# Hybrid decoder block: two delta heads' keys and queries kept on chip, attention's outputs stored whole, convolution's zeros by ScalarE

## The chip, the cores and the metric

The kernel runs on one core of one Trainium2 chip. Its time is that of one launch in microseconds on the device, as a median of several runs. The profile is one further execution, recorded by the hardware profiler. In its rows PE is TensorE's matmuls, PEld its weight loads, DVE is VectorE, ACT ScalarE, POOL GpSimd, SP SyncE; SPq marks what SP issues, which here is nearly every DMA.

## The reference

One decoder block over 1024 tokens of width 1024 in float32: a norm, one input projection, two groups of heads side by side (8 heads of stick-breaking attention of width 64, 4 heads of gated DeltaNet of width 128), their norms and gates, one output projection, the residual and a last norm.

```python
h = rmsnorm(x, norm1_w[layer])
proj = jnp.einsum('btd,de->bte', h, w_in[layer])
sb_q, sb_k, sb_v, sb_z, g_q, g_k, g_v, g_z, g_b, g_a = jnp.split(proj, split_idx, axis=-1)
o_sb = stick_breaking_attention(to_heads(sb_q, SB_HEADS, SB_HEAD_DIM),
                                to_heads(sb_k, SB_HEADS, SB_HEAD_DIM),
                                to_heads(sb_v, SB_HEADS, SB_HEAD_DIM))
o_sb = rmsnorm(o_sb.transpose(0, 2, 1, 3), sb_norm_w[layer]).reshape(b, t_len, SB_WIDTH)
o_sb = o_sb * jax.nn.silu(sb_z)
qkv = jax.nn.silu(causal_depthwise_conv(jnp.concatenate([g_q, g_k, g_v], axis=-1), gdn_conv_w[layer]))
gq, gk, gv = jnp.split(qkv, 3, axis=-1)
gq = l2norm(to_heads(gq, GDN_HEADS, GDN_HEAD_DIM)).astype(x.dtype)
gk = l2norm(to_heads(gk, GDN_HEADS, GDN_HEAD_DIM)).astype(x.dtype)
o_gdn = gated_delta_chunked(gq, gk, gv, decay, beta)
o_gdn = rmsnorm(o_gdn.transpose(0, 2, 1, 3), gdn_norm_w[layer]).reshape(b, t_len, GDN_WIDTH)
o_gdn = o_gdn * jax.nn.silu(g_z)
mixed = jnp.concatenate([o_sb, o_gdn], axis=-1)
x = x + jnp.einsum('bte,ed->btd', mixed, w_out[layer])
return rmsnorm(x, final_norm_w)
```

The convolution has four taps along time: each output needs the three inputs before it, and the first three of a sequence are zeros.

## The kernel before

**A planner writes the order.** The kernel is built by streams (Python generators, started at the end of `block`) that yield whenever they wait. `interleave` picks the stream that may go on and has the lowest rank; for the engines other than TensorE, `Model` (lines 176 to 345) keeps a simulated clock. Every instruction is recorded with a modelled cost and a rank `ck.prio`; of those that are ready in the model, the one of the lowest rank is taken next (`Model.start`). The orders found so are fixed by dependencies, so each engine runs its instructions in just that order. SP is one such engine, "S": it issues the DMAs one after the other, 0.475 us each in the model, and one whose data isn't there holds up all behind it. Ranks are given in line 37: DELTA 0, WEIGHTS 2, BANK 5, WINDOW 10, OUTPUT 12, RESULT 20. Since each instruction is issued by one helper (`call`, line 363), all rows of the profile have that line; they are told apart by the names of their tiles.

**Precision.** Most matmuls are made of three with operands split in a high and a low part (`mm3`): xh and xl are the split input, weh and wel a split column of weights, wer the raw column, each loaded in two halves.

**Stages.** Up to some 73 us the first projections (attention's queries and values) run while the input comes in. Then `projections` works through the other columns in `ORDER`: G0 to G3 are a delta head's keys, queries and values (kinds 1, 0, 2), k0 to k3 attention's keys, z the gates. Its rank, 100, makes it fill TensorE wherever delta and attention have nothing to do. From 531 us the output projection follows: 8 blocks of 128 rows with the delta half of the weights (`products_delta`), then 8 with attention's half (`products_attention`).

**Delta heads.** `g_evac` (line 878) takes a column out of PSUM in two halves of 512 tokens: ScalarE copies it to pre, behind three columns that are zeros (half 0, VectorE's memset, line 885) or the last three of the half before (ScalarE); the four taps give ac, in one of two buffers tagged kt; GpSimd multiplies ac by its sigmoid. Heads 0 and 1 (`TURNED` = 2) store the result to g_s as it is. Heads 2 and 3 store keys and queries to g_s as well, and all three kinds turned, by VectorE's transpose and four DMAs to gt_s.

`delta_load` (line 991) fetches, for each head and half (a unit), keys and queries from g_s into a slot kq of [128, 4 chunks, 2, 128]. There are four such slots; in the beginning they hold the raw input xr0 to xr3, and at the end the block inputs mg. `gdn_pre` turns keys and queries of heads 0 and 1 on TensorE (tile kw, the same bytes as kq), takes their norms (nkv) and the products kqf; it fetches its decays as cb and dt. All units' decays are computed ahead of the first unit, in the same stream. `gdn_chain` is the scan over the chunks, which ends with four stores to og_s.

**Attention.** `window` handles 256 queries of one head. z = q·k goes through sigmoids and a scan (sg, cc), is turned, split (ahl) and multiplied with the head's values v2a, a single tile loaded anew for each head when the last window of the head before has used it. The result, o2, is turned in 32x32 blocks by VectorE into oe, [128, 256], and stored to o_s by four DMAs of 32 partitions, 128 bytes a run, so that o_s holds token rows. Queries, keys high and low are loaded per head as q, kh, kl from qk_s; `k_evac` writes the keys there through the one tile sqh and a kt buffer, and `z_evac` uses the same two tiles.

**After attention.** `out_norm` loads one block of 128 rows from o_s (512 KB, whole rows) into a tile named both, adds the two halves of each head, and computes the norms. Its loads wait until the last window's stores are recorded. The loads for the delta half of the output projection (mgf from og_s and gate_s), the weights (worf) and x again (xr) run on SP in the same time.

Of the kernel before, what the change touches and what calls it, by code (L numbers as in the profile page):

```python
# [10 lines left out]
F32 = mybir.dt.float32  # L11
F32R = mybir.dt.float32r
I32 = mybir.dt.int32
AF = mybir.ActivationFunctionType
ALU = mybir.AluOpType
AX = mybir.AxisListType

P = 128
T = 1024
# [3 lines left out]
SBH = 8  # L23
# [8 lines left out]
TURNED = 2  # L32
# [1 line left out]

OUT_WEIGHTS, DELTA, WEIGHTS, BANK, WINDOW, OUTPUT, RESULT, DECAYS = -1, 0, 2, 5, 10, 12, 20, 25


SAME = 130  # L40
# [438 lines left out]
def block(tc, xT_d, x_d, n1_d, wE_d, wQ_d, wC_d, conv_d, alog_d, dtb_d, mixw_d, wo_d, fnw_d, out_d):  # L479
    nc = tc.nc  # L480
    ck = Model({"V": nc.vector, "A": nc.scalar, "G": nc.gpsimd, "P": nc.tensor, "S": nc.sync})
    V, A, G, TE, S = ck.V, ck.A, ck.G, ck.P, ck.S

    with ExitStack() as top:
        top.enter_context(tc.manual_schedule(engines={mybir.EngineType.PE}))

        def open_pool(name, space="SB", ctx=top, before=(), **kw):
            if space != "SB":
                kw["space"] = getattr(bass.MemoryType, space)
            return Pool(ck, ctx.enter_context(tc.tile_pool(name=name, bufs=1, **kw)), space, before)  # L490

        fx = Fixed(ck, nc, {**{f"sg{w}": (2048 * (w + 1), 1) for w in range(4)}, "o2": (1024, 1), "kq": (4096, 4), "ak": (4096, 4)})
        cst = open_pool("cst")
        dr = open_pool("dr", "DRAM")
# [13 lines left out]
        step = stepr.bitcast(F32)  # L508
# [7 lines left out]
        half = cst.tile([P, SBH], F32, name="half")  # L516
# [5 lines left out]
        def rsqrt(y, a, n):  # L522
            return G.tensor_tensor(y, a, half[:, 0:n], ALU.pow)
# [10 lines left out]
        gate_s = dr.tile([NK, P, T], F32, name="gate_s")  # L534
        g_s = dr.tile([GH, 3, P, T], F32, name="g_s")
        gt_s = dr.tile([GH, 3, T, P], F32, name="gt_s")
        o_s = dr.tile([T, SBH, P], F32, name="o_s")
        og_s = dr.tile([NB, P, GH, P], F32, name="og_s")
        rs_s = dr.tile([NB, P], F32, name="rs_s")
        cum_s = dr.tile([2, GH, NB, P], F32, name="cum_s")  # L540
# [16 lines left out]
        def turned(tp, parts):  # L557
            ck.hold(tp)
            for u, a in enumerate(parts):
                if a.dtype == F32R:  # L560
                    TE.transpose(tp[:, u * P:(u + 1) * P].bitcast(F32R), a, idr)
                else:
                    TE.transpose(tp[:, u * P:(u + 1) * P], a, ident)
            ck.free(tp)
            yield from ()
# [58 lines left out]
        for tag, bufs in (("kh", 1), ("kl", 1), ("q2", 1), ("v2a", 1), ("sg2", 1), ("cc", 2), ("cc", 2), ("sg3", 1)):  # L624
            if tag[0] == "s":
                chl.append(fx.tile([P, 2, 520], F32R, "chl", tag))
            else:
                t = at_.tile([P, 1040 + (48 if tag == "kl" else 0)], F32R, tag=tag, bufs=bufs, name="chl")
# [15 lines left out]
        raw, loads = [], {}  # L644
        for k in range(NK):
            w = s0.tile([P, 512], F32, tag="wcr", bufs=6, name="wq")
# [76 lines left out]
        def first(f, *args, bank=BANK, **kw):  # L723
            ck.prio, prio = bank, ck.prio
            f(*args, **kw)
            ck.prio = prio
# [49 lines left out]
        flags = {}  # L776
# [88 lines left out]
        def z_evac(i):  # L865
# [9 lines left out]

            return evac

        def g_evac(h, kind):
            wv = conv[:, 4 * kind + h, :]
            last = []  # L880

            def evac(pt, half):
                pre = gd.tile([P, 515], F32, tag="pre", bufs=2, name="pre")
                if half == 0:
                    V.memset(pre[:, 0:3], 0.0)
                else:
                    A.activation(pre[:, 0:3], last[0][:, 512:515], AF.Copy)
                last.append(pre)
                first(A.activation, pre[:, 3:515], pt, AF.Copy)
                ac = pr.tile([P, 512], F32, tag="kt", bufs=2, name="ac")  # L890

                first(A.activation, pt, pre[:, 0:512], AF.Copy, scale=wv[:, 0:1])
                for i in range(1, 4):
                    first(V.scalar_tensor_tensor, ac if i == 3 else pt, pre[:, i:i + 512], wv[:, i:i + 1], pt, ALU.mult, ALU.add)
                sg = pre[:, 0:512]
                first(A.activation, sg, ac, AF.Sigmoid)
                first(G.tensor_tensor, ac, ac, sg, ALU.mult)
                ts = slice(half * 512, half * 512 + 512)
                if h < TURNED:
                    return S.dma_start(g_s[h, kind, :, ts], ac)  # L900
                done = [S.dma_start(g_s[h, kind, :, ts], ac)] if kind < 2 else []
                first(V.transpose, sg, ac)
                turned = gt_s[h, kind, ts, :].rearrange("(b r) d -> r b d", r=32)
                return done + [S.dma_start(turned[:, :, 32 * a:32 * a + 32], sg[32 * a:32 * a + 32, :].rearrange("r (b c) -> r b c", c=32)) for a in range(4)]

            return evac

# [83 lines left out]
        def delta_load():  # L991
            yield lambda: "dec" in flags
            for h in range(GH):
                for g in range(2):
                    u = 2 * h + g
                    gst[h, g] = {}
                    half = "" if g else ".0"
                    yield lambda: u < 4 or f"c{u - 4}" in flags
                    if u > 3:
                        yield flags[f"c{u - 4}"]  # L1000
                    kq = fx.tile([P, 4, 2, P], F32, "kq", "kq")
                    ts = slice(512 * g, 512 * g + 512)
                    loads = []
                    for kind in (1, 0):
                        yield lambda: f"G{h}{kind}{half}" in flags
                        loads.append(S.dma_start(kq[:, :, 1 - kind, :], g_s[h, kind, :, ts].rearrange("p (c t) -> p c t", c=4)))
                    ak = fx.tile([P, 2, 4, P], F32, "ak", "ak")
                    kn, at = ak[:, 0], ak[:, 1]
                    nkv = gd.tile([P, 4, P], F32, tag="nkv", bufs=4, name="nkv")
                    gst[h, g].update(kq=kq, kn=kn, nkv=nkv, at=at)  # L1010
                    ck.hold(kq, kn, nkv)
                    turned = lambda kind: gt_s[h, kind, ts, :].rearrange("(c t) d -> t c d", t=P)
                    if h >= TURNED:
                        loads += [S.dma_start(kn, turned(1)), S.dma_start(nkv, turned(0))]
                    flags[f"l{u}g"] = loads
                    yield lambda: f"G{h}2{half}" in flags and (u == 0 or f"q{u - 1}" in flags)
                    vt = gd.tile([P, 4, P], F32 if h >= TURNED else F32R, tag="vt", name="vt")
                    flags[f"v{u}g"] = S.dma_start(vt, turned(2)) if h >= TURNED else S.dma_start(vt.rearrange("p c t -> p (c t)").bitcast(F32), g_s[h, 2, :, ts])
                    gst[h, g].update(vt=vt)
# [307 lines left out]
        def window(h, w, tok):  # L1327
# [3 lines left out]
            for i in range(2):  # L1331
                b = 2 * w + i
                end = (b + 1) * P
                sg = sg2[:, i, :]
                cc = ccs[i][:, T - end:T + 1]
                cuts = (0, 384, end) if end == 640 else (*range(0, end, 512), end)
                for s0, s1 in list(zip(cuts, cuts[1:]))[::-1]:
                    n = s1 - s0
# [19 lines left out]
            for j in range(w + 2):  # L1358
                if j <= w:
# [3 lines left out]
                    n = len(blocks)  # L1363
# [11 lines left out]
                    r = V.tensor_tensor(al, src, ah.bitcast(F32), ALU.subtract)  # L1375
# [13 lines left out]
                ahl, r = parts[j - 1]  # L1389
                ov2 = ov.rearrange("p (m t) -> p m t", m=2)  # L1390
                yield r
                for s in (2 * (j - 1), 2 * (j - 1) + 1):
                    i0 = 0 if s <= 2 * w else 1
                    c = slice(256 * (s % 2), 256 * (s % 2) + (1 if i0 else 2) * P)
# [10 lines left out]
            busy["po"] = 0  # L1405
            oe = at_.tile([P, 256], F32, tag="oe", bufs=2, name="oe")
            V.transpose(oe, o2)
            rows_o = o_s[256 * w:256 * w + 256, h].rearrange("(b r) d -> r b d", r=32)
            flags[f"e{h}{w}"] = [S.dma_start(rows_o[:, :, 32 * a:32 * a + 32], oe[32 * a:32 * a + 32].rearrange("r (b c) -> r b c", c=32)) for a in range(4)]
            yield  # L1410


# [2 lines left out]
        def out_norm(n):  # L1415
            yield lambda: f"e{SBH - 1}3" in flags and fx.room("sg3")
            if n == 0:
                fx.part("sg3", 4096)
            for b in range(n, NB, 2):
                yield lambda: fx.room("sg3")  # L1420
                both = fx.tile([P, SBH, 2, SBD], F32, "both", "sg3")
                ck.hold(both)
                yield S.dma_start(both.rearrange("p h u d -> p (h u d)"), o_s[b * P:(b + 1) * P].rearrange("t h d -> t (h d)"))
                o, spare = both[:, :, 0, :], both[:, :, 1, :]
                V.tensor_tensor(o, o, spare, ALU.add)
                A.activation(spare, o, AF.Square)
                ss = at_.tile([P, SBH], F32, tag="oss", bufs=2, name="oss")
                V.tensor_reduce(ss, spare, AX.X, ALU.add)
                V.tensor_scalar(ss, ss, 1.0 / SBD, EPS, ALU.mult, ALU.add)
                rsqrt(ss, ss, SBH)  # L1430
                normed[b] = both, o, ss
                yield
# [203 lines left out]
        pre = Stream(delta_pre(), 0.7, DELTA + 0.7)  # L1636
# [43 lines left out]
```

## Time and profile before

| | |
|---|---|
| runs shown | 636.03, 637.17, 634.78 us, median 636.03 |
| the profiled execution | 639.53 us; its span from first to last instruction 637.8 us |
| mean granted TensorE clock | 0.994 |
| instructions | 11259 |
| DMA | 165563 packets, 120.21 MB, 188 GB/s in the mean; 96448 packets under 512 B |

The span leaves out what lies around the first and the last instruction, 1.7 us. A busy PE in this profile isn't PE at its peak: matmuls overlap, and the end of each is modelled. In the views quoted below, a row of a tile gives the engine, the operation, its count, and min/median/max in ns with the first and last start; a row of the timeline gives the start, the duration and the instruction, with the idle time before it and who ended it in brackets; a row of waits gives who waited for whom, the sum, how often and the longest.

### The profile page before, as it was taken

To read this page: it belongs to the slowest core of one execution; us is meant where nothing else is said; L and a number is where in the kernel's file an instruction comes from. 1 tells how busy PE (TensorE), PEld (TensorE's weight loads), DVE (VectorE), ACT (ScalarE), POOL (GpSimd) and SP (SyncE) were. 2 spreads that over 40 slices of the span, in tenths; PEclk is the share of its full clock that TensorE was granted. 3 is DMA by queue.
4 is the path that set the end of the run, shared out by engine and by line. 5 is a ranking of instruction groups with operands and counts; after the bars stand their busy time and mean duration, and the time that the engine had idled before them with its cause. 6 is when DMAs were issued, how large, how long until landed. Compare 5 with 4: busy or idle time off the path is not lost.

```text
span 637.8 us, 11259 instructions
## 1 busy us (share of the span) xinstructions
PE 624.0 (98%) x3672; PEld 528.7 (83%) x3672; DVE 447.5 (70%) x810; ACT 393.9 (62%) x945; POOL 341.2 (53%) x429
## 2 busy tenths in 40 slices
PE   8999999999999999999999989999999999999995
PEld 7889988988888888788888777888888888888884
DVE  4379973322797798887797696777889774478754
ACT  6665567724786776775785866666777653232553
POOL 0124047728794696881679684386764325245522
PEclk9999999999999999999999999899999999999998
DMA  8958337856557466598668768453652578984322
GB/s 305 342 183 312 124 131 253 303 189 222 159 151 224 131 185 134 141 207 221 167 146 224 185 133 264 121 185 94 180 141 84 151 201 255 311 319 143 116 100 100
DMA packets 165563, 120.21 MB, mean 188 GB/s; under 512 B 96448, under 2 KB 131456, under 8 KB 165504
## 3 DMA queue, kind: packets, MB, share of 16 engines
q1 hardware_dynamic: 165216, 119.29, 62.3%
q8 instruction: 29, 0.48, 0.3%
q14 instruction: 30, 0.25, 0.1%
q10 hardware_dynamic: 288, 0.20, 0.1%
HBM read 80.22 MB, written 39.23 MB: 187 GB/s over the span
## 4 chain that ended last, share of the span: by engine, by line
PE 81%; DMA 6%; ACT 4%; DVE 3%; SPq 2%; issue 2%; POOL 1%; POOLq 0%; DVEq 0%; ACTq 0%
PE pp L363 52%; PE pz L363 21%; PE po L363 6%; PE pc L363 3%; SPq L363 2%; DVE cc L363 1%; DMA v2a<-v_s 1%; DMA kh<-qk_s 1%; DMA xr1f<-xT 1%; DMA o_s<-oe 1%; ACT sgf L363 1%; POOL ac L363 1%; DMA qk_s<-sqh 1%; ACT pz L363 1%; DMA cb<-cum_s 1%
## 5 line engine op out<-in xcount | busy, mean ns | idle before, releaser
L363 PE MATMUL pp<-xh,weh 128*128 128x512 f32 x360 | 146.4, 407 | 0.4 <-DVE ac L363 0.4
L363 PE MATMUL pp<-xh,wel 128*128 128x512 f32 x360 | 141.8, 394 | 0.0
L363 PE MATMUL pp<-xl,weh 128*128 128x512 f32 x360 | 141.3, 392 | 0.0
L363 POOL TENSOR_TENSOR sgf<-sgf,cc 128x128 f32<-128x128 f32 (+3 forms) x64 | 77.5, 1216 | 57.7 <-DVE cc L363 52.5
L363 POOL TENSOR_TENSOR wel<-wer,weh 128x512 fp32r<-128x512 f32 x48 | 62.5, 1305 | 72.0 <-ACT weh L363 71.6
L363 PEld LDWEIGHTS pp<-xh,wel 128*128 128x128 f32 x360 | 68.0, 189 | 15.3
L363 PEld LDWEIGHTS pp<-xh,weh 128*128 128x128 f32 x360 | 68.1, 189 | 12.8 <-DVE ac L363 0.9
L363 PEld LDWEIGHTS pp<-xl,weh 128*128 128x128 f32 x360 | 68.1, 189 | 11.5
L363 DVE TENSOR_TENSOR_SCAN cc<-pz,step 128x384 f32<-128x384 f32 (+2 forms) x64 | 53.4, 844 | 10.6 <-ACT pz L363 9.5
L363 ACT ACTIVATE sgf<-pz,rs 128x384 f32<-128x384 f32 (+3 forms) x96 | 53.5, 593 | 7.6 <-PE pz L363 7.6
L363 DVE TENSOR_TENSOR ahl<-pz,ahl 128x512 fp32r<-128x512 f32 (+1 forms) x80 | 49.5, 630 | 12.0 <-ACT ahl L363 11.3
L363 ACT ACTIVATE ahl<-pz 128x512 fp32r<-128x512 f32 (+1 forms) x80 | 43.2, 559 | 20.6 <-PE pz L363 20.1
L363 ACT ACTIVATE pz<-pz,ns 128x384 f32<-128x384 f32 (+3 forms) x96 | 52.5, 576 | 0.0
L363 PE MATMUL po<-ahl,v2a 128*128 128x512 f32 (+1 forms) x160 | 48.9, 400 | 2.4 <-DMA v2a<-v_s 2.3
L363 PE MATMUL pp<-wo,mmf 128*128 128x512 f32 x192 | 45.5, 396 | 0.0
L363 DVE SCALAR_TENSOR_TENSOR pp<-pre,conv,pp 128x512 f32<-128x512 f32 x42 | 31.4, 747 | 18.2 <-ACT pp L363 17.8
L363 PEld LDWEIGHTS pp<-wo,mmf 128*128 128x128 f32 x192 | 35.8, 188 | 8.4
L363 PE MATMUL pp<-woh,mmf 128*128 128x512 f32 (+2 forms) x136 | 41.9, 385 | 0.0
L363 DVE TENSOR_TENSOR_SCAN cc<-pz,cc,step 128x512 f32<-128x512 f32 (+1 forms) x32 | 38.8, 1211 | 4.1 <-ACT pz L363 3.0
L363 POOL TENSOR_TENSOR mmf<-mgf,mmf 128x512 fp32r<-128x512 f32 x16 | 21.9, 1366 | 37.0 <-ACT mmf L363 23.9
L363 POOL TENSOR_TENSOR ac<-ac,pre 128x512 f32<-128x512 f32 x24 | 31.0, 1293 | 16.3 <-ACT pre L363 10.9
L363 DVE TENSOR_TENSOR xr<-pp,xr 128x512 f32<-128x512 f32 (+2 forms) x33 | 22.2, 672 | 23.0 <-PE pp L363 23.0
(317 smaller groups left out, 1513.9 us busy)
## 6 DMA issues: line engine op xcount, KB each, us to landing
wer<-wE SPq DMA_DIRECT2D x48, 256.0 KB, 3.5
xr<-x SPq DMA_DIRECT2D x16, 512.0 KB, 7.6
g_s<-ac SPq DMA_DIRECT2D x20, 256.0 KB, 2.3
v_s<-v2e SPq DMA_DIRECT2D x16, 256.0 KB, 3.3
kqf<-g_s SPq DMA_DIRECT2D x16, 256.0 KB, 4.0
v2a<-v_s SPq DMA_DIRECT2D x8, 512.0 KB, 5.9
q<-qk_s SPq DMA_DIRECT2D x8, 512.0 KB, 4.5
kh<-qk_s SPq DMA_DIRECT2D x8, 512.0 KB, 3.9
```

The costliest lines, as they stand in the source:

```text
L363: ins = f(*args, **kw).ins
```

## The change

Five edits, in four places:

1. A new rank, STORES = 1.
2. Keys and queries of heads 0 and 1 are no longer stored to g_s and loaded again. `operand(h, g)` hands out the slot kq of a unit when its first product is made, and GpSimd's product writes straight into it, with a stride. The values of these heads go to g_s as before.
3. The stores of heads 2 and 3 (to g_s and gt_s) get the rank STORES in place of RESULT.
4. o_s is laid out as [4 windows, 8 heads, 128, 256]: a window's result oe is stored as it stands, by one DMA with 1 KB a partition. The order by token is made by the loads of `out_norm`: four for a block, each for 32 partitions, 128 bytes a run.
5. The three zero columns of pre are written by ScalarE, copied from a tile that holds zeros (step).

```diff
-OUT_WEIGHTS, DELTA, WEIGHTS, BANK, WINDOW, OUTPUT, RESULT, DECAYS = -1, 0, 2, 5, 10, 12, 20, 25
+OUT_WEIGHTS, DELTA, STORES, WEIGHTS, BANK, WINDOW, OUTPUT, RESULT, DECAYS = -1, 0, 1, 2, 5, 10, 12, 20, 25
...
-        o_s = dr.tile([T, SBH, P], F32, name="o_s")
+        o_s = dr.tile([4, SBH, P, 256], F32, name="o_s")
...
+        operands = {}
+
+        def operand(h, g):
+            if (h, g) not in operands:
+                operands[h, g] = fx.tile([P, 4, 2, P], F32, "kq", "kq")
+                ck.hold(operands[h, g])
+            return operands[h, g]
...
                 if half == 0:
-                    V.memset(pre[:, 0:3], 0.0)
+                    A.activation(pre[:, 0:3], step[:, 0:3], AF.Copy)
...
+                ts = slice(half * 512, half * 512 + 512)
+                if h < TURNED and kind < 2:
+                    kq = operand(h, half)
+                    ck.prio, prio = BANK, ck.prio
+                    r = G.tensor_tensor(kq[:, :, 1 - kind, :], ac.rearrange("p (c t) -> p c t", c=4), sg.rearrange("p (c t) -> p c t", c=4), ALU.mult)
+                    ck.prio = prio
+                    return r
                 first(G.tensor_tensor, ac, ac, sg, ALU.mult)
-                ts = slice(half * 512, half * 512 + 512)
                 if h < TURNED:
                     return S.dma_start(g_s[h, kind, :, ts], ac)
+                ck.prio, prio = STORES, ck.prio
                 done = [S.dma_start(g_s[h, kind, :, ts], ac)] if kind < 2 else []
                 first(V.transpose, sg, ac)
                 turned = gt_s[h, kind, ts, :].rearrange("(b r) d -> r b d", r=32)
-                return done + [S.dma_start(turned[:, :, 32 * a:32 * a + 32], sg[32 * a:32 * a + 32, :].rearrange("r (b c) -> r b c", c=32)) for a in range(4)]
+                done += [S.dma_start(turned[:, :, 32 * a:32 * a + 32], sg[32 * a:32 * a + 32, :].rearrange("r (b c) -> r b c", c=32)) for a in range(4)]
+                ck.prio = prio
+                return done
...
-                    kq = fx.tile([P, 4, 2, P], F32, "kq", "kq")
+                    kq = operand(h, g)
...
-                        loads.append(S.dma_start(kq[:, :, 1 - kind, :], g_s[h, kind, :, ts].rearrange("p (c t) -> p c t", c=4)))
+                        loads.append(flags[f"G{h}{kind}{half}"] if h < TURNED else S.dma_start(kq[:, :, 1 - kind, :], g_s[h, kind, :, ts].rearrange("p (c t) -> p c t", c=4)))
...
-            rows_o = o_s[256 * w:256 * w + 256, h].rearrange("(b r) d -> r b d", r=32)
-            flags[f"e{h}{w}"] = [S.dma_start(rows_o[:, :, 32 * a:32 * a + 32], oe[32 * a:32 * a + 32].rearrange("r (b c) -> r b c", c=32)) for a in range(4)]
+            flags[f"e{h}{w}"] = S.dma_start(o_s[w, h], oe)
...
-                yield S.dma_start(both.rearrange("p h u d -> p (h u d)"), o_s[b * P:(b + 1) * P].rearrange("t h d -> t (h d)"))
+                loads = []
+                for q in range(4):
+                    at = 32 * (4 * (b % 2) + q)
+                    loads.append(S.dma_start(both[32 * q:32 * q + 32].rearrange("p h u d -> p (h u d)").rearrange("p (n c) -> p n c", c=32),
+                                             o_s[b // 2, :, :, at:at + 32].rearrange("h (a r) c -> r (h a) c", r=32)))
+                yield loads
```

More of the change, by code (lines that the diff above doesn't have):

```diff
@@ L1010, in delta_load @@
                     gst[h, g].update(kq=kq, kn=kn, nkv=nkv, at=at)
-                    ck.hold(kq, kn, nkv)
+                    ck.hold(kn, nkv)
                     turned = lambda kind: gt_s[h, kind, ts, :].rearrange("(c t) d -> t c d", t=P)
```

## The prediction

> **What bounds the kernel now.** I read the page first, its busy times and the shares of the chain that ended last.
>
> ```profile
> PE 624.0 (98%) x3672; PEld 528.7 (83%) x3672; DVE 447.5 (70%) x810; ACT 393.9 (62%) x945; POOL 341.2 (53%) x429
> ...
> PE 81%; DMA 6%; ACT 4%; DVE 3%; SPq 2%; issue 2%; POOL 1%; POOLq 0%; DVEq 0%; ACTq 0%
> ```
>
> The reader sees a kernel that TensorE bounds: 13.8 of 637.8 us are all that it stands idle, and no part of the change removes a matmul. What can be won is inside the waits, so the view of waits for PE comes next (who waited for whom, total us, times, longest).
>
> ```profile
> PE po L363 <- DMA v2a<-v_s: 2.3, 1, 2.3
> PE po L363 <- DVE step L363: 1.7, 1, 1.7
> PE pz L363 <- ACT wy L363: 1.5, 1, 1.5
> PE pz L363 <- DVE cc L363: 0.6, 2, 0.4
> PE pp L363 <- DVE ac L363: 0.4, 1, 0.4
> PE pz L363 <- ACT nkv L363: 0.3, 1, 0.3
> PE pz L363 <- DVE state L363: 0.2, 1, 0.2
> ```
>
> The second row is the start of the kernel, which the change doesn't touch. The other six sum to 5.3 us: the whole pool that earlier data can empty. 3.8 us of it are two waits, and for these I asked the timeline of SP (the queue that issues nearly all DMAs, one after the other) and the chain in order of time (start us, us, what).
>
> ```profile
> 348.71 2.15 SPq L363 DMA_DIRECT2D o_s<-oe  x4
> ...
> 361.87 0.38 SPq L363 DMA_DIRECT2D v2a<-v_s  x1
> ```
>
> ```profile
> 351.21 0.83 PE po L363 x4
> ...
> 361.87 7.05 DMA v2a<-v_s
> ...
> 386.12 6.74 DMA kh<-qk_s
> ...
> 397.40 0.60 ACT wy L363
> ```
>
> The first wait: the single v2a tile was read for the last time at 352.04 (351.21 + 0.83), but the load of the next head's values is issued at 361.87, 9.8 us later. In between SP doesn't wait: from the first of the two rows of SP to the second stand 13 more rows with 17 DMAs, none over 0.11 us after the one before. SP itself is the bound there, at some half a microsecond for each DMA, and the load lands late by 2.3 us. The second wait has another cause: a store from the one sqh tile is issued when the load of kh has landed, ScalarE waits until that store lands, and the copy wy, which TensorE wants, stands behind it on ScalarE. After it the clock is low:
>
> ```profile
> 396.00:398.00 2.00, 0.59 (x4) 1.00 0.59 174
> 398.00:400.00 2.00, 1.95 (x6) 0.65 1.07 289
> 400.00:402.00 2.00, 2.00 (x6) 0.50 0.85 237
> ```
>
> (stretch, its length, PE busy and count, granted clock, DMA share, GB/s). At 0.65 and 0.50 of the clock, 2 us hold 1.3 and 1.0 us of work, so the dip cost 0.7 + 1.0 = 1.7 us.
>
> **The change part by part.** Rows of SP's DMAs (duration of one issue, min/median/max ns) and of their landing (KB each, median us):
>
> ```profile
> L363 SPq DMA_DIRECT2D o_s<-oe x128: 302/448/2572, 177.3 to 522.9; - x128
> L363 SPq DMA_DIRECT2D bothf<-o_s x8: 320/332/422, 514.9 to 590.4; - x8
> ...
> L363 SPq DMA_DIRECT2D g_s<-ac x20: 319/330/751, 88.7 to 339.8; - x20
> L363 SPq DMA_DIRECT2D kqf<-g_s x16: 371/434/522, 91.2 to 380.6; - x16
> ...
> L363 SPq DMA_DIRECT2D xc<-xd x4: 451/452/1042, 183.1 to 471.0; - x4
> ...
> bothf<-o_s SPq DMA_DIRECT2D x8, 512.0 KB, 6.2
> ...
> xc<-xd SPq DMA_DIRECT2D x4, 128.0 KB, 3.9
> ```
>
> *Attention's stores.* 128 quarter stores become 32 whole ones: 96 x 0.448 = 43 us less of SP's time between 177 and 523. What it is worth is read at the v2a wait. Of the 13.2 us from 348.71 on in which SP never rests, the four o_s issues take 2.15; one takes a quarter, 0.54. The load is then issued 1.6 us earlier and the wait falls from 2.3 to 0.7: **-1.6 us** (bounds 0 and -2.3). At the second wait SP pauses ahead of kh for a weight buffer, so o_s has no part in when kh is issued; fewer small packets beside kh's 6.74 us may shorten its flight. Bounds 0 and -1.5, taken **-0.5**, nearer to the end at which the cause stays. The clock dip hangs on that wait and on the thin matmuls before it; gone or not, 0 or -1.7, taken at half: **-0.9**.
>
> [...]
>
> *Delta's keys and queries of heads 0 and 1.* 8 stores and 8 loads go: 8 x 0.330 + 8 x 0.434 = 6.1 us of SP and 16 x 256 KB = 4 MB. The product that took their place is the same POOL instruction with a strided output, and the last two rows are the zeros:
>
> ```profile
> L363 POOL TENSOR_TENSOR ac<-ac,pre x24: 1266/1294/1344, 87.4 to 363.6; 128x512 f32<-128x512 f32 x24
> L363 POOL TENSOR_TENSOR kqf<-kqf,cb x8: 1267/1288/1299, 120.9 to 406.1; 128x512 f32<-128x512 f32 x8
> ...
> L363 DVE MEMSET pre<- x12: 61/61/61, 76.3 to 337.2; 128x3 f32 x12
> L363 ACT ACTIVATE pre<-pre x12: 186/234/268, 81.7 to 356.0; 128x3 f32<-128x3 f32 x12
> ```
>
> The second row writes with just that stride: 0 us for the 8 products. Each frees its buffer (kt) at its own end and not when a store has landed, which nothing waits for in this stage. The keys are there sooner by the landings of a store and a load, but is anything waiting for them?
>
> ```profile
> 100.49 0.43 SPq L363 DMA_DIRECT2D kqf<-g_s  x1
> ...
> 109.59 0.42 SPq L363 DMA_DIRECT2D cb<-cum_s  x1
> ...
> 109.86 0.80 PE L363 MATMUL pz<-step,kwf 128*128 128x128 f32 x8
> ```
>
> No: the transposes of the first unit come at 109.86, with the first load of its own decays (cb), more than 9 us after its last queries were asked for. The stream computes all decays first. So **0 us**, at best the 0.3 of the nkv wait, at worst 0. The slots are claimed earlier; their former owners, x's tiles, are read last before the first delta column.
>
> *Zeros by ScalarE.* 12 x 0.234 = 2.8 us on ScalarE, 12 x 0.061 = 0.7 off VectorE. Each stands in front of the bank's first copy, which waits for the same buffer, so no new wait; ScalarE has 244 us to spare. Bounds 0 and +2.8, taken **0**: TensorE waited for a convolution only once, 0.4 us.
>
> *The scattered loads.* 8 whole loads become 32, each with 128-byte runs. The xc load has exactly that form (128 KB, 32 floats a run): 0.452 a piece, so 14.5 us of SP in place of 8 x 0.332 = 2.7, and a block lands after 3 x 0.45 + 3.9 = 5.3 us against 6.2. A block's loads wait for the same eight heads' stores as now, and the delta blocks' loads stand behind them on SP. What they delay:
>
> ```profile
> 514.90 0.86 SPq L363 DMA_DIRECT2D bothf<-o_s  x2
> ...
> 524.24 0.34 SPq L363 DMA_DIRECT2D mgf<-og_s  x1
> ...
> L363 PE MATMUL pp<-wo,mmf x192: 388/395/473, 538.4 to 583.9; 128*128 128x512 f32 x192
> ...
> 531.73 1.29 POOL L363 TENSOR_TENSOR mmf<-mgf,mmf 128x512 fp32r<-128x512 f32 x1 [2.65 <-ACT mmf L363]
> ...
> 551.74 1.29 POOL L363 TENSOR_TENSOR mmf<-mgf,mmf 128x512 fp32r<-128x512 f32 x1 [5.28 <-DMA mgf<-gate_s]
> ...
> 577.43 1.27 DVE L363 SCALAR_TENSOR_TENSOR wol<-worf,mixw,woh 128x1024 fp32r<-128x1024 f32 x1
> ```
>
> The first two blocks' eight issues push the delta blocks' loads back by 8 x 0.452 - 0.86 = 2.8 us, less what the o_s stores ahead give back. Block 0's operand is ready at 533.0 and used at 538.4: 5.4 us of cover. A block takes (583.9 - 538.4)/8 = 5.7 us; block 4's operand is ready at 553.0 for 561.2, 8.2 us; the last weight at 578.7 for the attention products after 583.9, over 5. All covers are above 2.8, so **0 us**, and some +3 if they were used up.
>
> *Priorities and the order.* Stores of heads 2 and 3 get rank 1 in place of 20, ahead of weight loads (2) and attention's loads (10). All engines' orders are worked out anew from the model's costs, so no wait of today need come back at its place. No row shows this. Bounds by the pool of waits: -5.3 (none left) and +5.3 (as much again). Taken 0, the pool being nearly as small as it can be.
>
> Sum: -1.6 - 0.5 - 0.9 = -3.0 us. The profiled execution took 639.53 us, span 637.8 and 1.7 around it; it would become 636.5. The timed median lies 3.5 us lower, at 636.03, so some of these waits may be smaller in a timed run; I carry the sum over whole: **633.0 us**, 0.5% faster.
>
> **The rivals.**
>
> *It is hidden anyway: 636.0.* For it: TensorE's busy share, that of the eight heads' v2a loads only one made it wait, and the excess of the profile over the median, which may be these very waits. Against it: SP's unbroken row ahead of 361.87. [...]
>
> *More than forecast: 629.* A new order leaves none of the six waits and no dip: 636.0 - 5.3 - 1.7 = 629.0. For it: 88 fewer DMAs in all. Against it: the waits on VectorE and ScalarE have nothing to do with DMAs.
>
> *Slower: stores first, 641.*
>
> ```profile
> SPq L363 <- POOL ac L363: 18.1, 11, 5.2
> ...
> L363 SPq DMA_DIRECT2D gt_s<-pre x48: 303/488/1761, 231.3 to 369.8; - x48
> ```
>
> SP issues in order, and a store that is queued before its data exist holds all behind it. Already at rank 20 SP waited 11 times for a convolution's product, 1.6 us on average. At rank 1, 12 groups of heads 2 and 3 (four turned stores, and for two kinds of three one more) cost 4 x 0.488 + 0.33 = 2.3 us each, with the wait 3.9 us, ahead of loads of v2a, q, kh, kl. Where the load has no slack, as at 361.87, all 3.9 are TensorE's. It decides from the second group that does so: 2 x 3.9 less the 3.0 won is +4.8, 641. Against it: these stores stood in front of the loads in the old order too (four of the 17 DMAs above).
>
> **How the numbers follow.** Chances: forecast 0.50, hidden 0.17, more 0.15, slower 0.18. This kernel's measurement tells about 0.5%, 3.2 us, from no change: 632.85 to 639.21. The forecast lies at that edge, so half of it (0.25) counts as faster, with 0.15: 0.40. Same: 0.25 + 0.17 + 0.02 of the slower case: 0.44. Slower: 0.16. The range goes from the rival of 629 to that of 641; in its own case the forecast's range is 630.5 to 636.
>
> **What would show it.** Right: SP's row ahead of each v2a load is shorter and the v2a wait under 1 us; PE idle under 11 us; granted clock 1.00 in the middle; no PE wait after 515 us. Wrong in the term of the stores: v2a is still issued 9 us after its last reader. Wrong in the tail: PE waits for mmf between 538 and 590. Slower by the rival: SP waits for POOL ac or DVE pre over 25 us in sum, with a PE wait for kh, q or v2a behind them. What the trace of before can't tell is the new order.

## The result and the profile after

| | before | after |
|---|---|---|
| median of 7 runs each, on one chip | 637.17 us (634.78 to 638.02) | 641.09 us (639.36 to 643.96) |
| ratio, 95% interval | | 1.0062 [1.0043, 1.0081] |
| the profiled execution, its span | 639.53, 637.8 us | 640.94, 639.1 us |

The change made the kernel slower, by 3.9 us. Before's profiled execution was above all seven of its runs here and after's lay near its median, so the two profiles differ by less (1.4 us) than the runs do.

The page of after, busy times and shares of the chain:

```profile
PE 623.3 (98%) x3672; PEld 529.0 (83%) x3672; DVE 448.2 (70%) x798; ACT 395.7 (62%) x957; POOL 345.9 (54%) x429
...
PE 79%; DMA 5%; ACT 3%; POOL 3%; DVE 3%; SPq 3%; issue 2%; POOLq 0%; ACTq 0%; DVEq 0%
```

TensorE is as busy as before and stands idle 639.1 - 623.3 = 15.8 us in place of 13.8. The view of waits for PE in after (sum in us, times, longest):

```profile
PE po L363 <- DVE step L363: 1.7, 1, 1.7
PE pz L363 <- DVE cc L363: 1.6, 1, 1.6
PE pz L363 <- ACT pz L363: 1.4, 1, 1.4
PE pz L363 <- DVE dt L363: 1.2, 1, 1.2
PE pz L363 <- DMA kl<-qk_s: 1.1, 1, 1.1
PE pp L363 <- POOL wel L363: 0.7, 1, 0.7
PE pz L363 <- DVE xinv L363: 0.7, 2, 0.5
PE po L363 <- DMA v2a<-v_s: 0.4, 1, 0.4
PE pp L363 <- DVE v2e L363: 0.3, 1, 0.3
```

The wait for v2a fell from 2.3 to 0.4 and that for wy is gone. But six of the nine rows were not there before (of the others, the start of the kernel, cc and v2a, cc has grown from 0.6 to 1.6). Without the start they sum to 7.4 us against 5.3. So waits were not only removed; new ones came, at other places. The stretches around two of them, after (stretch, length, PE, PEld, DVE, ACT and POOL busy with counts, granted clock, DMA share, GB/s):

```profile
240.00:260.00 20.00, 18.81 (x106) 15.91 (x104) 13.90 (x25) 11.29 (x27) 11.12 (x11) 1.00 0.88 233
260.00:280.00 20.00, 17.86 (x109) 14.47 (x110) 15.08 (x29) 13.63 (x47) 17.09 (x23) 1.00 0.76 177
280.00:300.00 20.00, 20.00 (x160) 16.40 (x157) 14.29 (x29) 13.71 (x42) 10.65 (x13) 0.91 0.71 199
```

```profile
240.00:260.00 20.00, 20.00 (x114) 17.08 (x113) 16.54 (x29) 14.18 (x35) 11.69 (x20) 1.00 0.68 158
260.00:280.00 20.00, 19.59 (x100) 16.19 (x99) 17.60 (x34) 16.66 (x51) 17.79 (x18) 1.00 0.71 154
280.00:300.00 20.00, 20.00 (x203) 16.82 (x201) 15.10 (x31) 11.26 (x31) 9.21 (x12) 1.00 0.77 202
```

The second fence is the same view of before, where these 40 us cost 0.4 us of idleness. After lost 1.2 + 2.1 there, and 9% of the clock behind it. How the first of these waits came about is in the chain in order of time of after (start us, us, what):

```profile
252.16 5.19 DMA gt_s<-pre
...
257.74 0.71 ACT pre L363 x2
...
259.10 0.26 ACT kqf L363
259.35 0.49 ACT ahl L363
259.84 0.29 ACT pz L363 x2
...
260.17 0.50 PE pz L363 x2
```

A turned store of a delta head flies 5.19 us; ScalarE wants its buffer (pre) for the next column, and the copies that stand behind that in ScalarE's order, up to the one that frees a pz bank, are late with it. Of the two instructions that the chain merges as ACT pre, the first is the new copy of the zeros; ScalarE's timeline in after:

```profile
257.74 0.20 ACT L363 ACTIVATE pre<-step 128x3 f32<-128x3 f32 x1 [2.85 <-DMA gt_s<-pre]
257.85 0.58 ACT L363 ACTIVATE pre<-pp 128x512 f32<-128x512 f32 x1
```

The copy behind it (pre<-pp) is as in before and needs the same buffer: in before it is the instruction that waits for such a store, 0.81 us at 261.07. With before's order and the zeros by ScalarE (old_order_zeros, below) the wait is 0.88. So the zeros only stand at the head of this wait; that it has grown to 2.85 us goes with the new order.

The sign that I had set for the rival of stores first is absent. SP's waits in after:

```profile
SPq L363 <- POOL ac L363: 9.9, 4, 4.0
SPq L363 <- DVE pre L363: 8.2, 7, 2.6
```

That is 18.1 us in sum, under the bound of 25; in before the same two rows are 18.1 and 2.5, 20.6 in sum. Of the signs of a right forecast, two came (the v2a wait under 1 us, no wait of PE after 515 us) and two did not (PE idle under 11 us, the clock at 1.00 in the middle).

### The profile page after: what moved, and what is told of

It is laid out like the page before. It is cut to its first block, busy times and chain, and to the rows that moved or that the text cites. A ratio compares the mean times of both kernels' runs of the same rounds, so it can differ in the third digit from the quotient of the medians.

```text
span 639.1 us, 11148 instructions
## 1 busy us (share of the span) xinstructions
PE 623.3 (98%) x3672; PEld 529.0 (83%) x3672; DVE 448.2 (70%) x798; ACT 395.7 (62%) x957; POOL 345.9 (54%) x429
## 4 chain that ended last, share of the span: by engine, by line
PE 79%; DMA 5%; ACT 3%; POOL 3%; DVE 3%; SPq 3%; issue 2%; POOLq 0%; ACTq 0%; DVEq 0%
PE pp L363 49%; PE pz L363 21%; PE po L363 6%; PE pc L363 3%; SPq L363 3%; DMA wer<-wE 1%; DMA br<-bd 1%; DMA v2a<-v_s 1%; DMA gt_s<-pre 1%; POOL xs L363 1%; DMA qk_s<-sqh 1%; POOL tm L363 1%; DVE cc L363 1%; DMA og_s<-akf 1%; ACT pre L363 0%
## 5 line engine op out<-in xcount | busy, mean ns | idle before, releaser
L363 POOL TENSOR_TENSOR wel<-wer,weh 128x512 fp32r<-128x512 f32 x48 | 63.8, 1333 | 83.0 <-ACT weh L363 82.6
L363 ACT ACTIVATE ahl<-pz 128x512 fp32r<-128x512 f32 (+1 forms) x80 | 44.0, 558 | 18.1 <-PE pz L363 17.1
L363 PE MATMUL pz<-kh,q 128*128 128x384 f32 (+3 forms) x96 | 36.2, 383 | 1.4 <-ACT pz L363 1.4
L363 PEld LDWEIGHTS pz<-step,stf 128*128 128x128 f32 x288 | 31.7, 141 | 5.5 <-issue 0.2
```

What stands on the lines that cost most here:

```text
L363: ins = f(*args, **kw).ins
```

## The experiments

Each ratio is against before, timed on the same chip in the same job, with its 95% interval; before's own medians in the four jobs were 636.9, 637.45, 637.23 and 637.59 us. The ratio is the one on record, and not always the quotient of the two medians (for only_keys that would be 1.0168); where a ratio is given in us here, it is times 637.

### One part of the change at a time

Each kernel has one part of the diff and the rest of before; the planner draws each order anew.

```diff
# only_rank: the STORES rank around the stores of heads 2 and 3, nothing else
+                ck.prio, prio = STORES, ck.prio
# only_zeros
-                    V.memset(pre[:, 0:3], 0.0)
+                    A.activation(pre[:, 0:3], step[:, 0:3], AF.Copy)
# only_keys: operand(h, g) and the product into the slot
# only_store: o_s as [4, SBH, P, 256], one store a window, four loads a block
```

> Only the keys and queries of heads 0 and 1 are written straight into their slots; all orders are worked out anew from the changed costs. Theory A (the loss of 3.9 us is that of a newly drawn order, whatever edit caused the draw): any time from 633 to 642, with PE waits at other places than before; ratio between 0.995 and 1.008, no relation to the 6 us of SP time saved. Theory B (the stores of heads 2 and 3 at rank 1 hold up the loads): 635 to 637.5, as before. Theory C (the zeros on ScalarE make it wait for the pre buffer): 635 to 637.5.

> Only attention's results are stored whole and ordered by the loads. Theory A: any time from 633 to 642. Theory B and C: at or below before, 633 to 637. My prediction's term: -1.6 us at the v2a wait. The rival of the tail (scattered loads late): PE waits between 538 and 590 us, +3.

> Only the rank of the stores of heads 2 and 3 is 1 in place of 20; no instruction is added or taken away. Theory B: +3 to +5 us, 639.5 to 642, with SP waiting for POOL ac and DVE pre over 25 us and loads late behind it. Theory A: any time from 633 to 642, and SP's waits for ac and pre no more than before. Theory C: as before, 635 to 637.5.

> Only the three zero columns are written by ScalarE. Theory C: +2 to +4 us, 639 to 641, with a PE wait behind a ScalarE wait for the gt_s stores. Theory A: any time from 633 to 642. Theory B: as before, 635 to 637.5.

| | median us | ratio |
|---|---|---|
| only_keys | 647.59 | 1.0141 [1.0107, 1.0175] |
| only_store | 635.67 | 0.9972 [0.9948, 0.9996] |
| only_rank | 642.04 | 1.0067 [1.0042, 1.0092] |
| only_zeros | 645.26 | 1.0115 [1.0086, 1.0144] |

The four come to +9.0, -1.8, +4.3 and +7.3 us: +18.8, where all together cost 3.9. Parts that don't add up are no prices of parts. only_keys and only_zeros passed even theory A's ranges (633 to 642). only_rank has not one operation more, less or other than before, only another order, and that costs 4.3 us. Its longest waits for PE:

```profile
PE pz L363 <- DVE wy L363: 3.8, 1, 3.8
PE po L363 <- DVE step L363: 1.7, 1, 1.7
PE pp L363 <- ACT mmf L363: 1.5, 1, 1.5
PE pp L363 <- DVE kt L363: 1.5, 1, 1.5
```

In before neither VectorE's wy nor the tail's mmf nor kt was late. One half of the sign of stores first is here, SP's waits:

```profile
SPq L363 <- POOL ac L363: 25.4, 12, 7.9
SPq L363 <- DVE pre L363: 2.6, 4, 1.3
```

They come to 28.0 us, over the bound of 25. (redraw_before, below, has 39.7 us without the new rank, so this half alone says little.) The other half isn't here: no load of attention is among the waits of PE, and the longest, 3.8 us, lies behind VectorE, by its timeline:

```profile
288.38 3.43 DVE L363 TENSOR_TENSOR kqf<-kqf,norms 128x512 f32<-128x512 f32 x1 [3.04 <-POOL norms L363]
291.85 0.42 DVE L363 COPY wy<-pz 32x256 f32<-32x256 f32 x1
```

The first of these, work of a delta head, takes 0.69 us in the median of this kernel's eight, and 3.43 here. Three GpSimd instructions ran beside it, from 288.30 to 291.27; that they held it up is read from the times and not shown by a run. If they did, it is one way in which an order alone can cost time: it decides what runs beside what.

The zeros of only_zeros, 12 copies of 0.2 us, can't cost 7.3 us by themselves either.

### The order or the work?

Two ways to part them. One draws a new order for unchanged work, by a constant of the planner; the other keeps an order and changes the work. For the second, the planner is told of the old instruction (`planned` records it with its cost, but issues nothing) and the new one is put into its place in the engine's order:

```diff
# redraw_before: before's work, another draw
-SAME = 130
+SAME = 135
# redraw_after, redraw2_after: after's work, two more draws
-SLACK = 450
+SLACK = 470
...
-            cost = 475
+            cost = 480
# old_order_all: all changed work, each engine in before's order (here the stores of a window)
+            whole = [nc.sync.dma_start(o_s[w, h], oe).ins]
+            flags[f"e{h}{w}"] = [planned(ck, "S", [] if a else whole, "dma_start", ...) for a in range(4)]
# zeros_order_old_work: the planner is told of only_zeros' copy, VectorE's memset is issued
+                    zeros = nc.vector.memset(pre[:, 0:3], 0.0).ins
+                    planned(ck, "A", [], "activation", pre[:, 0:3], step[:, 0:3], AF.Copy)
```

SAME, SLACK and the cost of an issue only steer the planner; none is an instruction. In zeros_order_old_work the memset is put directly ahead of VectorE's first tap.

> All the changed work (keys and queries straight into the slots, whole stores, loads by token, zeros by ScalarE), but every engine keeps the order of the kernel before: the planner is still told of the old instructions, and those that no longer exist leave a gap in its lists. Theory A (the loss is the new order's, the work itself is no dearer): 632 to 637, at or below before; the v2a wait near 0.7 us and no new PE wait over 1 us. Theory B (the rank) says the same, for the rank is part of the order. Theory C (the zeros make ScalarE wait): 639 or more. Theory D (the work itself costs 4 us, by the scattered loads or by ScalarE's longer queue): 639 or more, PE waits behind both, mmf or pre.

> The other way round: the instructions of the kernel before, zeros by VectorE, but every engine in the order that the planner drew when the zeros were ScalarE's (the kernel with only the zeros changed took 645.3 us). Theory A: 643 to 646, as slow as that kernel. Theory C: back to 636 to 638, since ScalarE has no instruction more.

> The kernel before with one constant of the planner changed: an engine's own next instruction may start 135 ns after the last one in the model, not 130. No instruction differs, but the orders are drawn anew about as widely as with the single edits. Theory A: another time than before's by some us, as likely slower, 634 to 646. Theories B, C, D: 636 to 638.

> The changed kernel with one constant of the planner changed (the slack before a stream goes on, 470 ns and not 450): the orders are drawn anew, the work is the same. Theory A: some us away from 641, either side, 634 to 648. Theories B, C, D: 640 to 642, since rank, zeros and work are all there.

> The changed kernel with another constant of the planner changed (an issue of SP costs 480 ns in the model, not 475). Order theory: another draw, anywhere from 634 to 648 and away from 641 by over 1 us as likely as not. If the changed work set the time: 640 to 642.

| work | order | median us | ratio |
|---|---|---|---|
| before's | only_rank's | 642.04 | 1.0067 [1.0042, 1.0092] |
| before's | redraw_before's | 644.76 | 1.0109 [1.0081, 1.0138] |
| before's | only_zeros' | 649.13 | 1.0192 [1.0155, 1.0229] |
| changed | after's | 641.09 | 1.0062 [1.0043, 1.0081] |
| changed | redraw_after's | 638.16 | 1.0014 [0.9994, 1.0034] |
| changed | redraw2_after's | 635.87 | 0.9975 [0.9957, 0.9993] |
| changed | before's | 639.19 | 1.0028 [1.0010, 1.0046] |

The third row is no pure draw. It took 3.9 us more than only_zeros, whose order it keeps, and lies above the 643 to 646 expected. The late memset adds a wait that neither before nor only_zeros has (ScalarE's tap for VectorE's memset):

```profile
ACT pp L363 <- DVE pre L892: 9.3, 9, 1.8
```

So its 12.2 us can't be put down to the order alone.

The order moves the time by more than the work does. Before's work, in the first two orders, took 4.3 and 6.9 us longer; the changed work in three new orders spans 635.87 to 641.09. redraw2_after, with the same rank STORES and the same operations as after, is faster than both kernels. Its longest waits, by the view for PE:

```profile
PE po L363 <- DVE step L363: 1.7, 1, 1.7
PE pz L363 <- DVE cc L363: 1.3, 1, 1.3
PE po L363 <- DMA v2a<-v_s: 1.0, 1, 1.0
```

and redraw_before's longest:

```profile
PE pp L363 <- ACT bothf L363: 2.2, 1, 2.2
PE po L363 <- DVE step L363: 1.7, 1, 1.7
PE pp L363 <- DVE wo L363: 1.6, 1, 1.6
PE pz L363 <- DVE state L363: 1.3, 1, 1.3
PE pz L363 <- DVE dt L363: 1.0, 2, 0.6
```

Each draw has its own list of who is late; before's list was one of them, a short one.

### What the changed work costs in the old order

old_order_all is 1.8 us slower than before in the order in which all of my durations had been read. That misses the 632 to 637 of theory A: the changed work is dearer too, and 1.5 us of PE's waits stand behind xr in the tail, as theory D had it. (Theory C gave the same time, by the zeros; they cost 0.4 us alone, below.) Its parts, by the same means:

> Only keys and queries straight into their slots, in the old order (with its own new order this edit took 647.6 us). Order theory: 636 to 638, no dearer than before, for 16 DMAs fall away and nothing is added. If the work itself were dear (a product that writes into slots waits for them, or POOL's strided write blocks VectorE): 640 or more.

> Only the zeros by ScalarE, in the old order (with its own new order this edit took 645.3 us). Order theory: 636.5 to 638.5, at most the 2.8 us of ScalarE's 12 copies. If ScalarE's wait for pre were the cost: 640 or more.

> Only the whole stores and the loads by token, every engine in the order of the kernel before. The profile of all changed work in the old order has a new PE wait at 576 to 580 us behind VectorE (xr), which waits there for the scattered loads of both (4.3 us in sum). If that is what costs 1.7 us there, this kernel is as slow as that one, 638.5 to 640, with the same wait. If the stores' saving of SP time is worth what I predicted, and the loads nothing: 634 to 636.

Keys: 639.09, 1.0021 [1.0003, 1.0039]. Zeros: 637.64, 1.0006 [0.9987, 1.0025]. Store with scattered loads: 640.00, 1.0040 [1.0015, 1.0065]. Keys lies between the ranges of its two theories. The three come to +4.3 us where all together cost 1.8; each interval is over 1 us wide to either side, so this doesn't show that they interact, and no part is known to better than that.

The same three edits also tell what a draw costs, for each was timed with its own new order and with the old one: keys 1.0141 and 1.0021 (+7.6 us by the draw), zeros 1.0115 and 1.0006 (+6.9), store 0.9972 and 1.0040 (-4.3).

What the last did in the tail, from the timelines of SP, VectorE and TensorE of old_order_store (start us, us, instruction, in brackets the idle time before it and who ended it):

```profile
574.31 9.24 SPq L1435 DMA_DIRECT2D bothf<-o_s  x8
...
582.82 0.69 DVE L363 TENSOR_TENSOR bothf<-bothf 128x512 f32<-128x512 f32 x1 [2.07 <-DMA bothf<-o_s]
583.42 0.68 DVE L363 TENSOR_TENSOR xr<-pp,xr 128x512 f32<-128x512 f32 x1
...
584.16 2.10 PE L363 MATMUL pp<-wo,mmf 128*128 128x512 f32 x8 [2.03 <-DVE xr L363]
```

Eight issues hold SP 9.24 us, 1.16 each where I had counted 0.452. VectorE keeps to its order and waits 2.07 us for that block; behind it stands xr, which takes a finished product out of PSUM, and TensorE has no free bank until then: 2.03 us. The two halves of this edit, stores and loads, were then parted:

```diff
# old_order_plain: whole stores, one plain load a block
+                loads.append(nc.sync.dma_start(both.rearrange("p h u d -> p (h u d)"),
+                    o_s[b // 2, 4 * (b % 2):4 * (b % 2) + 4].rearrange("h p c -> (h p c)").rearrange("(p n) -> p n", n=T)).ins)
# old_order_scatter: before's quarter stores, four scattered loads a block
+                o_w = o_s.rearrange("t h d -> (t h d)").rearrange("(w h p c) -> w h p c", w=4, h=SBH, p=P)
...
+                    loads.append(nc.sync.dma_start(both[32 * q:32 * q + 32].rearrange("p h u d -> p (h u d)").rearrange("p (n c) -> p n c", c=32),
+                                                   o_w[b // 2, :, :, at:at + 32].rearrange("h (a r) c -> r (h a) c", r=32)).ins)
```

> The whole stores in the old order as in old_order_store (1.0040), but a block of out_norm is fetched by one plain load of 512 KB with 4 KB a partition, in the place of the four scattered ones; the order by token is left out, so the norm's rows are mixed. Theory (the scattered loads are what costs in the tail): VectorE's waits for both fall back from 6.1 us to about the 0.5 of before, PE's wait for DVE xr (2.0 us) is gone, issues of both are near 0.33 us, and the time is 636 to 638, a ratio of 0.998 to 1.001. Rival (the store in one piece or the gaps in SP's row cost it): xr is still late by 1 us or more and the ratio stays at 1.003 to 1.005.

> The other half in the old order: before's four quarter stores for each window, and four scattered loads for a block, 128 bytes a run, in the place of the one whole load; they read the same bytes by the other layout, so the norm's rows are mixed. Theory (the scattered loads are what costs): PE waits 1.5 to 2 us for DVE xr at 575 to 582, VectorE 4 us or more for both, v2a is late by 2.3 us as before since the stores are as they were, and the time is 638.5 to 641, a ratio of 1.002 to 1.006. Rival (the loads are harmless without the whole stores): no wait for xr, ratio 0.999 to 1.001.

old_order_plain took 638.05 us, 1.0009 [0.9992, 1.0026]; old_order_scatter 640.40, 1.0049 [1.0025, 1.0072]. The loads are the cost, with or without the whole stores. Their issues, by the tile's view (count, ns min/median/max), of old_order_plain and of old_order_scatter:

```profile
L1433 SPq DMA_DIRECT2D bothf<-o_s x8: 319/332/423, 512.2 to 588.0; - x8
```

```profile
L1434 SPq DMA_DIRECT2D bothf<-o_s x32: 303/572/5547, 511.2 to 590.2; - x32
```

VectorE's waits for them, plain and scattered:

```profile
DVE bothf L363 <- DMA bothf<-o_s: 0.3, 1, 0.3
```

```profile
DVE bothf L363 <- DMA bothf<-o_s: 4.0, 4, 1.5
```

And one stretch of the tail (columns as above), plain and scattered:

```profile
560.00:580.00 20.00, 20.00 (x95) 16.19 (x94) 17.46 (x25) 7.41 (x10) 9.26 (x6) 1.00 0.71 246
```

```profile
560.00:580.00 20.00, 19.35 (x90) 15.33 (x89) 16.36 (x23) 6.49 (x9) 8.97 (x6) 1.00 0.99 234
```

With runs of 128 bytes the DMA engines were busy 0.99 of this stretch in place of 0.71, at 234 GB/s in place of 246; in the whole kernel an issue took 0.572 us in the median, against 0.332, and up to 5.5, and VectorE waited 4.0 us for the blocks, against 0.3 in old_order_plain. This profiled execution was the lowest of its twelve (637.1 us) and has only 0.7 us of wait for xr, less than the 1.5 to 2 expected. The cost is read from the ratio, the path from old_order_store's timeline.

## Why the prediction was wrong

**The step that failed** is "Priorities and the order", taken at 0 with bounds of -5.3 and +5.3, "the pool being nearly as small as it can be". That a small pool leaves little to win is right. But I read it as if it centred the term at 0, where a short list of waits is a reason to expect a longer one from another draw. And the pool is no bound above, since a new order makes waits that the old one hasn't. Measured with before's work: +4.3 and +6.9 us (ratios 1.0067 and 1.0109 times 637). With one edit each, against the same edit in the old order: +7.6, +6.9 and -4.3. With the changed work, against the old order's 1.0028: +2.2, -0.9 and -3.4. Of the eight kernels in a new order five are slower than before clear of noise, one is the same, two are faster. Of after's +3.9 us, 1.8 are thus the work in the old order and the rest, about 2, the draw. The split is one reading, as an edit's cost depends on the order too: in after itself no PE wait lies behind 515 us, though the scattered loads are there.

**The whole stores**, -3.0 us in three terms, were over-sized. The mechanism at v2a was there: the wait was 1.5 in old_order_all, 1.3 in old_order_plain, 0.4 in after, for a forecast of 0.7; with before's stores it was 1.9 to 2.8 in old_order_scatter, old_order_keys and old_order_zeros. The load was issued 0.9 us earlier in old_order_plain and 2.3 in old_order_store, for a forecast of 1.6. In old_order_store v2a no longer made TensorE wait, and a copy to nkv by ScalarE, 0.9 us, came last at the same matmul: the next wait was close behind, and I hadn't looked for it. Yet the time of old_order_plain is +0.6 us (-0.5 to +1.7) from before's. The three terms are worth nothing that shows in the median, as the rival "hidden" had it.

What took back the gain at v2a stays open. What the runs do show is that the other two terms, the second wait (for wy, -0.5) and the clock dip after it (-0.9), had no firm ground. The wait for wy, 1.5 us in before, is 0.3 in old_order_scatter and absent in old_order_keys, whose stores are before's. And that the dip hangs on it and on thin matmuls was my estimate; no run shows the -0.9. In before the clock stayed at 1.00 from 364 to 376 us, across a longer pause of TensorE, 2.33 us (the wait for v2a) against 1.46. In old_order_plain the wait for wy is gone, TensorE stands idle 0.35 us in all between 380 and 400, and the clock falls all the same, a little earlier (columns as above):

```profile
392.00:394.00 2.00, 2.00 (x25) 1.63 (x19) 1.89 (x5) 0.76 (x5) 0.00 (x0) 0.56 1.03 393
394.00:396.00 2.00, 2.00 (x15) 1.35 (x15) 0.44 (x1) 2.00 (x13) 0.22 (x1) 0.58 1.01 386
```

In old_order_scatter, in the same order, the clock is 1.00 from 380 to 400, where old_order_plain has 0.91 in the mean. The clock differs from run to run of the same kernel: of the 100 runs of before in the four jobs, the 27 with a mean clock of 0.994 took 637.8 us in the mean, the 23 with 0.997 636.1. I had taken all three terms from one execution of 639.53 us, above 91 of those 100, noted the 3.5 us between it and the median, and carried the sum over whole.

**The scattered loads**, 0 us, were mis-sized: +3.1 us in old_order_scatter (1.6 to 4.6), and 2.0 between old_order_store and old_order_plain. Two things were wrong in that term. The 0.452 us came from the rows of xc, four issues between 183 and 471 us; here 32 stand among the loads of mgf, worf and xr. And the covers were those of mmf and of the last weight alone; the one that ran out was VectorE's queue, where xr stands behind the block. The sign that I had named, PE waiting for mmf between 538 and 590, did not come; the wait had xr's name. In old_order_scatter an issue took 0.572 us in the median, beside 3.6 us from issue to landing, but four in a row held SP 8.31 us, 2.1 each; the row of its timeline:

```profile
551.25 8.31 SPq L1434 DMA_DIRECT2D bothf<-o_s  x4
```

**Keys and queries**, 0 us: +1.3 us in the old order (0.2 to 2.5). In old_order_keys the transposes of the first unit start at 110.0 us, against 109.86, so nothing was waiting for these keys, as forecast. What costs the 0.2% stays open. In its profile no wait for PE is longer than before's by over 0.2 us, and its span is 637.2 us against 637.8. Some 0.3 us of it lies outside the span: 2.0 us around the first and the last instruction in the mean of its runs, 1.7 in before's. The strided product costs what I took: 1.296 us in after, against 1.294.

**Zeros**, 0 us: held, +0.4 (-0.8 to +1.6).

**The rivals.** "Stores first" named nearly the right time, 641, by the wrong way: its sign is absent in after, only its half at SP came in only_rank, and with the same rank two other draws are at 638.16 and 635.87. "More" (629) was reached by no draw of eight; the best, only_store and redraw2_after, are 0.25 to 0.28% under before. The rival that was missing is a slower one in which the new order alone makes new waits. The range ended at 641, the time of stores first; by the runs with before's work and another order it should have gone some 3 us further (636.0 + 6.9), and more with an edit's own draw.

## What to carry to other kernels

Where a planner or scheduler redraws the order, an edit's time is one sample: price the draw as a term of its own, from the time of unchanged work under other planner constants, and if before's list of waits is short, expect that term to be positive more often than not (five of eight draws here). To judge the edit itself, hold the order and change the work, and to ship it, draw several orders. Price a DMA of short runs by an issue among the transfers that it will meet (here 1.16 us each for eight in the tail, where xc's rows had 0.452), and look for its cover in the queue of whoever consumes it in order, not only at the last operand.

## What the hardware showed that I had not expected

- The issue of a DMA on SP was no constant here. One with 128-byte runs (1024 of them) took 0.303 us at least and 5.8 us at most in one kernel, old_order_store, by its row in the view of the tile:

```profile
L1435 SPq DMA_DIRECT2D bothf<-o_s x32: 303/620/5767, 515.3 to 595.9; - x32
```

- The size of the reaction to order alone: the same operations took from 637 to 645 us, 1.1%, with TensorE 98% busy in before, so that a "full" engine says little about what another order can lose.
